# Decoder layer on one core: the seven products of a down part accumulate on copied-in sums and come in steps behind three tiles

## Chip, core and metric

The kernel runs on one core of a Trainium2 chip, as one program. The metric is the device time of one execution in microseconds (us). The core has a matrix engine (TensorE, PE in the profile, with its weight loads as PEld), a vector engine (VectorE, DVE), a scalar engine (ScalarE, ACT), GpSimd (POOL) and SyncE (SP). Each takes its instructions in the order in which they stand in its queue. In this kernel SP issues the plain transfers of the weights and POOL the others, among them transfers that add to what stands at their destination.

## The reference

One layer of a decoder: a SwiGLU block, a merge of attention and a linear recurrence, and a second SwiGLU block, each between two RMS norms. 512 tokens, model width 1024, 2816 hidden units in each SwiGLU block. The change touches the two SwiGLU blocks only:

```python
def swiglu(x, w_gate, w_up, w_down):
    return (jax.nn.silu(x @ w_gate) * (x @ w_up)) @ w_down

for l in range(DEPTH):
    f = swiglu(rms_norm(h, ffn1_norm_pre[l]), ffn1_w_gate[l], ffn1_w_up[l], ffn1_w_down[l])
    h = h + 0.5 * rms_norm(f, ffn1_norm_post[l])
    ...                      # attention, recurrence, merge
    f = swiglu(rms_norm(h, ffn2_norm_pre[l]), ffn2_w_gate[l], ffn2_w_up[l], ffn2_w_down[l])
    h = h + 0.5 * rms_norm(f, ffn2_norm_post[l])
```

## The kernel before

**Precision.** Every matrix product runs as three products of 32-bit operands that were split into a high and a low part (high times high, high times low, low times high). `split` (L277) makes the two parts of an operand: ACT copies the high part (L278), DVE subtracts it (L279). So each weight that the stream brings must pass ACT and DVE before PE can use it.

**Tiles and parts.** A SwiGLU block (`ffn`) has NF = 22 tiles f of 128 hidden units. The first ones (5 in the first block, 3 in the second) are plain products. From then on a tile is a `prod`: gate and up projection together, computed as a 2 by 2 block product with seven instead of eight block products (p1 to p7, `seven`, L592). One prod is 7 products of 12 matmuls of 256 columns (L603 to L605). Within it a partial sum b is copied to SBUF by ACT (`c`, L610) before the next product accumulates on it, and DVE forms the results g and u from PSUM and these copies (L615). The tiles fall into five parts (`FF_PARTS`): part 0 is tiles 0 to 3, parts 1, 2, 3 are four tiles each, part 4 is tiles 16 to 21.

**Down projection.** Part 0 and part 4 are projected down plainly. Parts 1 to 3 (`SEVEN`) use seven block products again: `down7` is called one tile late, behind tiles 8, 12 and 16. Its 14 groups (7 products, two token blocks each) of 6 matmuls of 512 columns (L783 to L785) go to PSUM. After each group ACT copies the partial sum to a tile `cs` (L789), and POOL issues one or two accumulating transfers (L791) that add it to the output sums `facc`: 16 for a part, 96 in the program. The seven operands on the weights' side are made by `d_forms` from two fetches of 1 MB, both ahead of tile 8 (12, 16); one sum is made by a further accumulating transfer (L743). Three of the seven are made in `rest`, in the middle of `down7`.

**What sets the order.** `ffn_order` writes the order of the events down; a scheduler then places the instructions on each engine, with priority for what is marked `high_priority`. The order of PE follows the events. The weights come as one stream in the order of `stream_plan`, at most 1 MB at a time, into two buffers `raw` (L222), issued by SP (L224). A fetch starts when the last instruction that reads the buffer's earlier content is done. The split weights stand in four tiles `w8` of [128, 2, 1024] and two `w4`. `w_forms` (L573) makes a prod's seven operands from 1 MB: four sums on DVE (L579, L580, L581, L584), three large splits and a small one; it takes three `w8`, so each waits until PE has used what stood there.

**PSUM.** Eight banks: five `acc`, three `aux`. A prod takes two `acc` and one `aux`.

**Other tiles named below.** The pool tag `wd` holds one tile: the split activations of tile 3 (`act3`) until part 0's down projection has run, and then the rows of gains for the norm behind the block, which POOL fetches (L409). The tag `tt` holds the unsplit forms of a down part's activations. `last_product` ends the block: part 4's down projection added to `facc`, and the norm. Its matmuls (L397 to L399) start behind tile 21; their weights go into spare tiles, `tx` among them.

## Time and profile before

| | |
|---|---|
| time, median of 3 runs | 1268.79 us (1265.55 to 1272.86) |
| the profiled execution's own time | 1275.29 us |
| its span, first to last instruction | 1273.5 us |
| busy: PE / DVE / ACT / POOL | 97% / 76% / 58% / 9% of the span |
| granted TensorE clock, mean | 0.987 |

The profile is one execution, 6.5 us above the median of the runs. Times within it count from the first instruction. A matmul's row shows more than the time from one start to the next, since matmuls overlap, so the pace of PE is read from starts. The first SwiGLU block's prods and down parts (tiles 5 to 21) stand at 82.65 to 328.87 us, the second's at 980.29 to 1226.30 us. In the view of waits, a line gives who waited for whom, the total, how often, and the longest. In the chain of waits each row is what the work that ended last was waiting for at that time.

### The profile page before, as it was taken

The numbers are of one execution on the slowest core, as the hardware profiler recorded it, in microseconds if no ns is written. First come the engines' busy times: TensorE is split into PE (matmuls) and PEld (weight loads), VectorE is DVE, ScalarE is ACT, GpSimd is POOL, SyncE is SP. The second block draws the span as 40 slices with busy tenths as digits, with TensorE's granted clock in tenths as the row PEclk, the third lists the DMA queues.
The fourth block names the chain that finished last, engine by engine and source line by source line (L and its number), as shares of the span: only waits on it lengthen the run. The fifth ranks groups of instructions, "written<-read, shape, count | busy, mean of one in ns | idle before, by whom it ended". The sixth has DMA issues, their size and how long they took to land.

```text
span 1273.5 us, 19380 instructions
## 1 busy us (share of the span) xinstructions
PE 1230.8 (97%) x7676; PEld 1114.4 (88%) x7676; DVE 971.4 (76%) x1521; ACT 735.1 (58%) x1214; POOL 113.4 (9%) x153
## 2 busy tenths in 40 slices
PE   9999999999999999999999999999999999989887
PEld 8889888989777899999988887888998989888886
DVE  7969697878577488888575888854885879787855
ACT  7546656565455455666543797634664575756442
POOL 0000314030002000000000000000100031313000
PEclk9999999999899999999999999999999999999889
DMA  6233859584535122222242222225533386858631
GB/s 237 100 105 111 198 150 209 140 199 134 196 116 158 66 108 80 96 77 98 98 167 99 94 74 97 102 97 182 161 122 115 103 204 153 202 140 187 157 133 66
DMA packets 42075, 169.72 MB, mean 133 GB/s; under 512 B 4608, under 2 KB 7808, under 8 KB 27904
## 3 DMA queue, kind: packets, MB, share of 16 engines
q1 hardware_dynamic: 20016, 122.86, 28.0%
q0 software_dynamic: 21968, 45.62, 16.5%
q8 instruction: 60, 0.98, 0.3%
q14 instruction: 31, 0.25, 0.1%
HBM read 129.67 MB, written 6.29 MB: 107 GB/s over the span
## 4 chain that ended last, share of the span: by engine, by line
PE 73%; DVE 12%; DMA 8%; ACT 5%; issue 2%; DVEq 0%; SPq 0%; ACTq 0%
PE acc L603 8%; PE acc L604 8%; PE acc L605 8%; DMA raw<-in_w 8%; PE acc L291 6%; PE acc L292 6%; PE acc L293 6%; DVE w L279 4%; PE acc L397 3%; PE acc L399 3%; PE acc L398 3%; PE acc L783 2%; PE acc L784 2%; PE acc L785 2%; PE aux L603 2%; PE aux L604 2%
## 5 line engine op out<-in xcount | busy, mean ns | idle before, releaser
L279 DVE TENSOR_TENSOR w<-raw,w 128x1024 fp32r<-128x1024 f32 (+1 forms) x279 | 304.0, 1094 | 105.5 <-ACT w L278 93.1
L278 ACT ACTIVATE w<-raw 128x1024 fp32r<-128x1024 f32 (+1 forms) x279 | 265.5, 954 | 155.4 <-PE acc L293 48.3
L603 PE MATMUL acc<-big,w 128*128 128x256 f32 x896 | 254.7, 284 | 0.6 <-ACT c L610 0.6
L604 PE MATMUL acc<-big,w 128*128 128x256 f32 x896 | 254.6, 284 | 0.0
L605 PE MATMUL acc<-big,w 128*128 128x256 f32 x896 | 254.1, 284 | 0.0
L603 PEld LDWEIGHTS acc<-big,w 128*128 128x128 f32 x896 | 172.1, 192 | 1.4 <-ACT c L610 0.9
L604 PEld LDWEIGHTS acc<-big,w 128*128 128x128 f32 x896 | 172.0, 192 | 0.4
L605 PEld LDWEIGHTS acc<-big,w 128*128 128x128 f32 x896 | 172.0, 192 | 0.0
L603 PE MATMUL acc<-tx,w 128*128 128x256 f32 x272 | 80.0, 294 | 24.1 <-ACT c L610 23.9
L791 POOL DMA_DIRECT2D facc<-cs x96 | 82.0, 872 | 152.7 <-ACT cs L789 75.8
L610 ACT ACTIVATE c<-acc 128x256 f32<-128x256 f32 x172 | 65.0, 378 | 49.8 <-PE acc L605 46.1
L603 PE MATMUL aux<-big,w 128*128 128x256 f32 x288 | 83.2, 289 | 0.0
L604 PE MATMUL aux<-big,w 128*128 128x256 f32 x288 | 83.1, 288 | 0.0
L605 PE MATMUL aux<-big,w 128*128 128x256 f32 x288 | 83.0, 288 | 0.0
L605 PE MATMUL acc<-tx,w 128*128 128x256 f32 x272 | 78.7, 289 | 0.0
L604 PE MATMUL acc<-tx,w 128*128 128x256 f32 x272 | 78.4, 288 | 0.0
L603 PEld LDWEIGHTS acc<-tx,w 128*128 128x128 f32 x272 | 53.5, 197 | 26.5 <-ACT c L610 26.5
L291 PE MATMUL acc<-big,w 128*128 128x512 f32 x192 | 74.7, 389 | 0.0
L292 PE MATMUL acc<-big,w 128*128 128x512 f32 x192 | 74.7, 389 | 0.0
L293 PE MATMUL acc<-big,w 128*128 128x512 f32 x192 | 74.7, 389 | 0.0
L579 DVE TENSOR_TENSOR s<-raw 128x512 f32<-128x512 f32 x52 | 35.9, 690 | 47.0 <-DMA raw<-in_w 46.9
L279 DVE TENSOR_TENSOR w<-s,w 128x1024 fp32r<-128x1024 f32 x52 | 63.5, 1221 | 2.8 <-ACT w L278 2.7
(352 smaller groups left out, 2982.7 us busy)
## 6 DMA issues: line engine op xcount, KB each, us to landing
raw<-in_w SPq DMA_DIRECT2D x110, 1024.0 KB, 4.8
facc<-cs POOLq DMA_DIRECT2D x96, 256.0 KB, 6.7
raw<-raw POOLq DMA_DIRECT2D x6, 512.0 KB, 4.4
big<-xf POOLq DMA_DIRECT2D x6, 512.0 KB, 4.5
gains<-in_rows POOLq DMA_DIRECT2D x5, 512.0 KB, 7.4
h<-in_x SPq DMA_DIRECT2D x8, 256.0 KB, 5.2
h<-in_xn POOLq DMA_DIRECT2D x4, 512.0 KB, 5.5
kept_m<-h POOLq DMA_DIRECT2D x4, 512.0 KB, 2.9
```

Of the source, the lines that this page charges most:

```text
L278: ACT.activation(dh, src, AF.Copy)
L279: DVE.tensor_sub(dl, src, dh.bitcast(F32))
L291: PE.matmul(ps, wh, xh, start=first, stop=False)
L292: PE.matmul(ps, wh, xl, start=False, stop=False)
L293: PE.matmul(ps, wl, xh, start=False, stop=last)
L397: PE.matmul(ps, x.hi[k][:, bl], wh, start=k == 0, stop=False)
L398: PE.matmul(ps, x.hi[k][:, bl], wl, start=False, stop=False)
L603: PE.matmul(ps, wh, xh, start=start and k == 0, stop=False, skip_group_check=True)
L604: PE.matmul(ps, wh, xl, start=False, stop=False, skip_group_check=True)
L605: PE.matmul(ps, wl, xh, start=False, stop=k == 3, skip_group_check=True)
L610: ACT.activation(c, ps, AF.Copy)
L791: nc.gpsimd.dma_start(fb(o + i, FHALVES[half]), c, accum_op=ALU.add)
```

## The change

Down7 is cut into three steps: products p1 and p7 behind the first tile of the next part, p4, p6 and p5 behind the second, p2 and p3 behind the third (`SEVEN_STEPS`). Each step fetches its own quarters of the weights (1 MB, 1 MB, 0.5 MB; the quarter u0 twice) and makes its operands on DVE (four additions a part instead of three and an accumulating transfer). The activations' forms are made together behind the part's fourth tile.

Nothing is accumulated by transfers any more. Each product has a sum in SBUF: p2, p3 and p4 have a quarter of `facc`, p1, p7, p6 and p5 have a place in a new tile `ea`. Ahead of a group ACT copies the sum into the PSUM bank (`seed`), the group's matmuls accumulate on it, and ACT copies it back. In part 1 the four products with a place in `ea` start from nothing. The first three seeds of a step are written ahead of the tile before it; each later one stands behind the copy back of the group that had the bank. Behind part 3, eight DVE additions of 128x1024 (`merge`) put the places in `ea` into `facc`: five behind its second step, three behind its third.

Down groups now use the three `aux` banks, part 0's too; a prod takes three `acc`. The fourth tile of part 0 moves to the tag `e`, and `wd` holds the steps' running sum `sum` of the weights, from part 1's first step to part 3's last. So the gains wait for that.

```diff
+SEVEN_STEPS = (("p1", "p7"), ("p4", "p6", "p5"), ("p2", "p3"))
+SEVEN_RAW = (("g0", "u0"), ("u1", "u0"), ("g1",))
...
 def ffn_order(n):
...
+    after = {FF_PARTS[a + 1][0] + i: (a, i) for a in SEVEN for i in range(len(SEVEN_STEPS))}
...
+        if f in after:
+            order.append(("prepd",) + after[f])
...
+        if f in after:
+            order.append(("seeds",) + after[f])
         order.append(("prod", f))
...
+        if f in after:
+            order.append(("down7",) + after[f])
...
-                for i in range(2):
-                    plan.append((("dg", n, ev[1], i), 2048))
+                for q in SEVEN_RAW[ev[2]]:
+                    plan.append((("dq", n, ev[1], q), 1024))
...
+            tt = x["tt"]
+            put(tt[:, i // 2 * 2:i // 2 * 2 + 2, i % 2, :], lambda ap: ap.rearrange("p (q t) -> p q t", q=2))
+            q = tt.rearrange("p q j t -> p q (j t)")
+
+            def pair(*ps):
+                v = f32r_big().rearrange("p (s c) t -> p s (c t)", s=2)
+                for k, p in enumerate(ps):
+                    x[p] = v[:, :, k * T:k * T + T]
+                return v
+
+            def form(v, src):
+                split(v[:, 0], v[:, 1], src)
+
+            if i == 1:
+                pair("p1", "p7")
+                form(x["p1"], q[:, 0])
+                DVE.tensor_sub(q[:, 0], q[:, 0], q[:, 1])
+            if i == 3:
+                with tc.high_priority(offset=AHEAD):
+                    DVE.tensor_sub(q[:, 1], q[:, 3], q[:, 1])
+                    form(x["p7"], q[:, 1])
+                    two = pair("p6", "p4")
+                    v = f32r_big().rearrange("p c t -> p (c t)")
+                    x["p5"] = v[:, 0:2 * T].rearrange("p (s t) -> p s t", s=2)
+                    form(x["p5"], q[:, 0])
+                    DVE.scalar_tensor_tensor(q[:, 0], q[:, 3], -1.0, q[:, 0], op0=ALU.mult, op1=ALU.subtract)
+                    DVE.scalar_tensor_tensor(q[:, 1], q[:, 0], -1.0, q[:, 2], op0=ALU.mult, op1=ALU.subtract)
+                    form(two, tt[:, 0:2].rearrange("p q j t -> p (q j t)"))
+                    form(pair("p2", "p3"), tt[:, 2:4].rearrange("p q j t -> p (q j t)"))
...
-                ps, y = acc_ps(), fb(b, FHALVES[half])
+                ps = aux_ps()
                 tokens(ps, ws, part(a), b)
-                if a == 0:
-                    ACT.activation(y, ps, AF.Copy)
-                else:
-                    DVE.tensor_add(y, ps, y)
+                ACT.activation(fb(b, FHALVES[half]), ps, AF.Copy)
 
         def prod(f, w):
             g, u = tmp("g"), tmp("u")
-            seven(t, w, aux_ps()[:, :HB], [g[:, h] for h in HALVES], [u[:, h] for h in HALVES])
+            seven(t, w, acc_ps()[:, :HB], [g[:, h] for h in HALVES], [u[:, h] for h in HALVES])
...
+        def d_forms(a, i):
+            x, w = sevens[a], {}
             def form(name, src):
                 w[name] = w8()
                 split(w[name][:, 0, :], w[name][:, 1, :], src)
             with tc.high_priority(offset=AHEAD):
+                raw = [raw_of(("dq", n, a, q)) for q in SEVEN_RAW[i]]
+                if i == 0:
+                    x["sum"] = apool.tile([P, 2, D], F32, name="sum", tag="wd", bufs=1)[:, 0, :]
+                sd = x["sum"]
+                if i == 0:
+                    g0, u0 = raw
+                    form("p1", g0)
+                    DVE.tensor_add(sd, g0, u0)
+                    form("p7", sd)
+                elif i == 1:
+                    u1, u0 = raw
                     form("p4", u1)
+                    DVE.tensor_add(sd, sd, u1)
+                    DVE.tensor_add(u0, u0, u1)
+                    form("p6", sd)
+                    form("p5", u0)
+                else:
+                    g1, = raw
+                    form("p2", g1)
+                    DVE.tensor_add(sd, sd, g1)
+                    form("p3", sd)
+            return w
...
+        outs = {"p2": (0, 0, 1.0), "p3": (2, 0, 1.0), "p4": (0, 1, -1.0)}
+        extra = ("p1", "p7", "p6", "p5")
+        seeded = {}
+        def quarter(o, half):
+            return facc.rearrange("p (b h) t -> p b h t", h=2)[:, o:o + 2, half, :]
+        def sum_at(p):
+            if p in outs:
+                o, half, sign = outs[p]
+                return quarter(o, half), sign
+            return acts["ea"][:, extra.index(p)], 1.0
+        def groups(i):
+            return [(p, k) for p in SEVEN_STEPS[i] for k in range(2)]
+        def seed(a, p, k):
+            if "ea" not in acts:
+                acts["ea"] = apool.tile([P, 4, 2, T], F32, name="ea", tag="e", bufs=1)
+            ps = seeded[p, k] = aux_ps()
+            if p in outs or a > SEVEN[0]:
+                src, sign = sum_at(p)
+                ACT.activation(ps, src[:, k], AF.Copy, scale=sign)
+        def down7(a, i, w):
+            x = sevens[a]
+            gs = groups(i)
+            for m, (p, k) in enumerate(gs):
+                ps = seeded.pop((p, k))
+                first = not (p in outs or a > SEVEN[0])
+                for j in range(2):
+                    xh, xl = (x[p][:, s_, j * HB + k * P:j * HB + k * P + P] for s_ in range(2))
+                    wh, wl = (w[p][:, s_, j * T:(j + 1) * T] for s_ in range(2))
+                    PE.matmul(ps, xh, wh, start=first and j == 0, stop=False, skip_group_check=True)
+                    PE.matmul(ps, xh, wl, start=False, stop=False, skip_group_check=True)
+                    PE.matmul(ps, xl, wh, start=False, stop=j == 1, skip_group_check=True)
+                dst, sign = sum_at(p)
+                with tc.high_priority(offset=EVAC):
+                    ACT.activation(dst[:, k], ps, AF.Copy, scale=sign)
+                    if m + 3 < len(gs):
+                        seed(a, *gs[m + 3])
+            if a == SEVEN[-1]:
+                merge(i)
+        def merge(i):
+            p1, p7, p6, p5 = (acts["ea"][:, k] for k in range(4))
+            if i == 1:
+                DVE.tensor_add(p6, p6, p1)
+                DVE.tensor_add(p7, p7, p6)
+                for p in (p7, p5):
+                    DVE.tensor_sub(quarter(2, 1), quarter(2, 1), p)
+                DVE.tensor_sub(quarter(0, 1), quarter(0, 1), p7)
+            if i == 2:
+                DVE.tensor_add(quarter(0, 0), quarter(0, 0), p1)
+                for p in (p6, p5):
+                    DVE.tensor_add(quarter(2, 0), quarter(2, 0), p)
...
+            elif ev[0] == "seeds":
+                for g in groups(ev[2])[:3]:
+                    seed(ev[1], *g)
...
             a = part_of(f)
             i = f - FF_PARTS[a][0]
-            if a:
-                if i % 2 == 0:
-                    acts[a, i // 2] = f32r_big()
-                at, i = acts[a, i // 2], i % 2
-            elif i == 3:
-                at, i = apool.tile([P, 4, T], F32R, name="act3", tag="wd", bufs=1), 0
...
```

The order on three engines. In these rows the number behind a tile's name is that of its buffer, and the line is that of the program the row is from: in the changed one L286 and L287 are the two halves of `split`, L587 to L592 the sums of `w_forms`, L618 and L623 the copies c and the sums g and u, L739 a tile's silu and L740 the product g times u behind it, L798 a seed, L814 a copy back, L824 to L832 the merges.

On DVE in the first block, before, around the first sum g of tile 20 (g_3127, from the bank acc_3131):

```order
L279 TENSOR_TENSOR w8_3114<-raw_3108,w8_3114 128x1024
L615 TENSOR_TENSOR g_3002<-aux_3004,c_3046 128x256
L584 TENSOR_TENSOR raw_3108<-s12_3110,raw_3108 128x512
L725 SCALAR_TENSOR_TENSOR u_3104<-g_3002,u_3003 128x512
L279 TENSOR_TENSOR w4_3117<-raw_3108,w4_3117 128x512
L615 TENSOR_TENSOR g_3127<-acc_3131,c_3144 128x256
```

And after, at the same sum (g_3115, from acc_3119):

```order
L287 TENSOR_TENSOR w8_3102<-raw_3096,w8_3102 128x1024
L830 TENSOR_TENSOR facc_79<-facc_79,ea_1134 128x2x512
L592 TENSOR_TENSOR raw_3096<-s12_3098,raw_3096 128x512
L287 TENSOR_TENSOR w8_3103<-s12_3098,w8_3103 128x1024
L832 TENSOR_TENSOR facc_79<-facc_79,ea_1134 128x2x512
L287 TENSOR_TENSOR w4_3105<-raw_3096,w4_3105 128x512
L287 TENSOR_TENSOR w8_3104<-raw_3096,w8_3104 128x1024
L832 TENSOR_TENSOR facc_79<-facc_79,ea_1134 128x2x512
L740 SCALAR_TENSOR_TENSOR u_3092<-g_2990,u_2991 128x512
L623 TENSOR_TENSOR g_3115<-acc_3119,c_3132 128x256
```

The sum g of tile 20 moved behind three merges and behind two more of tile 21's large splits. From the last split of tile 18's weights to this sum there stand 48 rows on DVE: 20 of 1024 columns a partition (8 of them merges), 19 of 512 and 9 of 256.

On ACT in the first block, before, from the last copy c of tile 21 (c_3306) on; g_3234 is tile 21's silu, tx_3473 a split of the last product's weights, xf_3231 the split of tile 21's activations:

```order
L610 ACTIVATE c_3306<-acc_3237 128x256
L278 ACTIVATE tx_3473<-raw_3468 128x1024
L724 ACTIVATE g_3234<-g_3234 128x512
L278 ACTIVATE act_3470<-raw_3468 128x1024
L278 ACTIVATE xf_3231<-u_3336 128x512
```

And after:

```order
L618 ACTIVATE c_3294<-acc_3225 128x256
L739 ACTIVATE g_3222<-g_3222 128x512
L286 ACTIVATE tx_3461<-raw_3456 128x1024
L286 ACTIVATE xf_3219<-u_3324 128x512
L286 ACTIVATE act_3458<-raw_3456 128x1024
```

The silu moved ahead of the split `tx` and the activations' split ahead of `act`; on DVE the product u behind the silu moved ahead of `tx` too. The second block ends in the same way.

On ACT in the first block, after, in the second step of part 2 (p4, p6, p5), from tile 13's silu on; sums are copied back and seeds copied in in turn with the forms of tile 14's weights:

```order
L739 ACTIVATE g_1970<-g_1970 128x512
L814 ACTIVATE facc_79<-aux_1964 128x512
L798 ACTIVATE aux_2084<-ea_1134 128x512
L814 ACTIVATE facc_79<-aux_1966 128x512
L286 ACTIVATE w8_1952<-s12_1947 128x1024
L798 ACTIVATE aux_2093<-ea_1134 128x512
L814 ACTIVATE ea_1134<-aux_1968 128x512
L286 ACTIVATE w4_1954<-raw_1945 128x512
L286 ACTIVATE w8_1953<-raw_1945 128x1024
L798 ACTIVATE aux_2102<-ea_1134 128x512
```

Before, ACT copied sums to `cs` between such forms and had no seeds. In the second step of parts 2 and 3 the last group, on the bank of the last seed above, stands on PE behind the first 5 matmuls of the next tile. On POOL the 48 transfers `facc<-cs` and 3 `raw<-raw` of each block are gone, and the gains are the only transfers there between a block's first tiles and its end.

More of the change, by code (lines that the diff above doesn't have):

```diff
@@ L646, in act_at @@
             i = f - FF_PARTS[a][0]
[L647 to L653 removed]
+            if a == 0:
                 if i == 0:
@@ L656, in act_at @@
                 at = acts[0]
+            else:
+                if i == 0:
+                    acts[a] = apool.tile([P, 4, T], F32R, name="act4", tag="tt", bufs=1)
+                elif i % 2 == 0:
+                    acts[a] = f32r_big()
+                at, i = acts[a], i % 2
             acts["at", f] = at[:, 2 * i, :], at[:, 2 * i + 1, :]
@@ L670, in into @@
                 u = tmp("u")
-                put(u)
+                put(u, lambda ap: ap)
                 split(*act_at(f), u)
@@ L694, in into @@
-            DVE.scalar_tensor_tensor(tt[:, 2, :], tt[:, 1, :], -1.0, u[:, :HB], op0=ALU.mult, op1=ALU.subtract)
-            x["t", j] = f32r_big().rearrange("p s t -> p (s t)").rearrange("p (s k t) -> p s k t", s=2, k=4)
-            split(x["t", j][:, 0], x["t", j][:, 1], tt)
+                sevens[a] = {"tt": apool.tile([P, 4, 2, HB], F32, name="tt", tag="tt", bufs=1)}
+            x = sevens[a]
+            tt = x["tt"]
+            put(tt[:, i // 2 * 2:i // 2 * 2 + 2, i % 2, :], lambda ap: ap.rearrange("p (q t) -> p q t", q=2))
@@ L708, in std_out @@
             DVE.tensor_mul(u, psu, r)
-            into(f, lambda dst: DVE.tensor_mul(dst, u, g))
+            into(f, lambda dst, v: DVE.tensor_mul(dst, v(u), v(g)))
         def down(a, half):
@@ L819, in ffn @@
             elif ev[0] == "down7":
-                down7(ev[1], *forms.pop("d"))
+                down7(*ev[1:], forms.pop("d"))
             else:
```

108 lines of the change are left out of this document (16 added, 92 removed).

## The prediction, made before the changed kernel ran

> **What bounds the kernel now.** I read the page first, then the stretch of each SwiGLU block from tile 5 to tile 21, then PE's waits in it, then the chain of waits behind one of them.
>
> ```profile
> PE 1230.8 (97%) x7676; PEld 1114.4 (88%) x7676; DVE 971.4 (76%) x1521; ACT 735.1 (58%) x1214; POOL 113.4 (9%) x153
> raw<-in_w SPq DMA_DIRECT2D x110, 1024.0 KB, 4.8
> facc<-cs POOLq DMA_DIRECT2D x96, 256.0 KB, 6.7
> ```
>
> PE is the bound. What is to be won is the time in which it waits. A weight fetch of 1 MB lands 4.8 us behind its issue (median).
>
> ```profile
> 82.65:328.87 246.22, 233.12 (x1681) 221.99 (x1680) 203.20 (x288) 150.67 (x238) 46.97 (x57) 0.99 0.66 170
> 980.29:1226.30 246.01, 234.51 (x1681) 223.03 (x1680) 202.58 (x287) 150.47 (x238) 46.28 (x56) 0.98 0.66 168
> 299.61 0.42 DVE L615 TENSOR_TENSOR g<-aux,c 128x256 f32<-128x256 f32 x1
> 309.69 0.41 DVE L615 TENSOR_TENSOR g<-aux,c 128x256 f32<-128x256 f32 x1
> 124.69 0.40 PE L783 MATMUL acc<-w,xf 128*128 128x512 f32 x1
> 143.76 0.28 PE L603 MATMUL acc<-big,w 128*128 128x256 f32 x1
> ```
>
> The first two rows are the stretches of tiles 5 to 21 in the two blocks: length, then busy time of PE, PEld, DVE, ACT, POOL. The next two are the last sums of two undisturbed tiles: a tile is 309.69 - 299.61 = 10.08 us of PE, so a product (a seventh) is 1.44. The last two are the first matmul of a down7 and the first behind it: 19.07 us for 14 groups, 1.36 a group. Seventeen tiles and three down7 make 17 x 10.08 + 3 x 19.07 = 228.6 us. The stretches take 246.2 and 246.0: **17.6 and 17.4 us are lost** in them.
>
> ```profile
> PE acc L603 <- ACT c L610: 13.0, 5, 3.3
> PE acc L603 <- ACT c L610: 11.4, 6, 3.7
> 226.00:229.40 3.40, 3.40 (x18) 3.40 (x17) 2.89 (x6) 1.85 (x4) 0.00 (x0) 0.50 1.02 292
> 229.40:232.80 3.40, 3.40 (x31) 3.40 (x30) 3.00 (x4) 1.72 (x3) 0.00 (x0) 1.00 0.30 54
> ```
>
> PE's waits in the two stretches are 13.0 us in 5 and 11.4 us in 6, nearly all on the copy c. Behind a wait of over 3 us the granted clock is 0.50 for a while: 18 matmuls instead of 31 in 3.40 us, which is 13 x 0.12 = 1.5 us more.
>
> ```profile
> 212.08 7.27 DMA raw<-in_w
> 219.38 0.70 DVE s L579
> ...
> 224.34 0.34 DVE g L615
> 224.71 0.63 ACT g L724
> 225.34 0.28 ACT c L610
> 212.56 0.85 POOL L791 DMA_DIRECT2D facc<-cs  x1 [0.37 <-issue]
> 213.83 0.85 POOL L791 DMA_DIRECT2D facc<-cs  x1 [0.42 <-DMA facc<-cs]
> ```
>
> The first five rows are the chain behind part 2's down7; they end a wait. The weights of tile 15 land after 7.27 us instead of 4.8. DVE has their sums in its queue ahead of tile 13's last sums, so those come late; ACT has tile 13's silu ahead of tile 14's copy c; PE waits for c. The fetch is late twice over: it starts late, since down7 held both buffers, and it shares the transfer engines with `facc<-cs`, which POOL issues at 212.56 and 213.83 (the last two rows).
>
> **What the change does, term by term.** The 96 accumulating transfers and their six sisters go, and with them the bursts: fetches should land in about 4.8 us. A part's 2 MB of down weights come in three fetches over three tiles, so no tile's fetch waits behind `rest`. I went through ACT, DVE and the buffers for parts 1 to 3 with the durations of this trace, and found each tile's weights split 2 us or more ahead of their first matmul. The waits behind down7 go with what follows them.
>
> ```profile
> 83.14 1.20 POOL L409 DMA_DIRECT2D gains<-in_rows  x2 [82.70 <-PE acc L399]
> 83.89 7.05 DMA raw<-in_w
> 96.92 0.28 ACT c L610
> ```
>
> The first wait of each stretch stands ahead of down7 (its c at 96.92) and comes from another neighbour: the gains are fetched at 83.14, and the weight fetch at 83.89 takes 7.05 us. Now the gains wait for the tag `wd`, until part 3's last step, so this one goes too. All of 17.6 and 17.4 goes, then; what comes in its place:
>
> (1) **Merges on DVE.** Eight additions a block.
>
> ```profile
> L754 DVE TENSOR_TENSOR raw<-sd,raw x6: 1221/1222/1222, 126.5 to 1150.6; 128x1024 f32<-128x1024 f32 x6
> 285.76 1.22 DVE L279 TENSOR_TENSOR w<-raw,w 128x1024 fp32r<-128x1024 f32 x1
> 286.89 0.42 DVE L615 TENSOR_TENSOR u<-acc,c 128x256 f32<-128x256 f32 x1
> 287.23 1.22 DVE L279 TENSOR_TENSOR w<-raw,w 128x1024 fp32r<-128x1024 f32 x1
> 295.23 0.69 DVE L580 TENSOR_TENSOR s<-s,raw 128x512 f32<-128x512 f32 x1
> 295.84 0.69 DVE L581 TENSOR_TENSOR raw<-raw 128x512 f32<-128x512 f32 x1
> ```
>
> An addition of 128x1024 in SBUF (L754) lasts as long as a large split, and from start to start a large split takes 286.89 - 285.76 = 1.13 us, a row of 512 0.61 and one of 256 0.34. From the last split of tile 18 to the first sum g of tile 20, the 48 rows on DVE take 20 x 1.13 + 19 x 0.61 + 9 x 0.34 = 37.2 us. They begin when the second group of p6 is done and ACT has made the high part (1.05, and 0.5 for what stands ahead of it). From that group on, PE has 2 groups, tile 18, 4 groups, tile 19 and five products of tile 20: 2.7 + 10.1 + 5.4 + 10.1 + 7.2 = 35.5 us, less 1.5 that DVE starts later, 34.0. The product p4 of tile 20 overwrites the bank that this sum g reads. So PE waits about **3.2 us** there; queued behind p4 is the rest of the tile. Without the merges (8 x 1.13 = 9.0) there would be 5.8 us to spare. Bounds: 0 if DVE falls back less, some 6 if its splits wait for ACT. I add 1.5 for the clock, as behind the wait that ended behind 225.34: 4.7 a block.
>
> The Trainium skill ("TensorE: Matmul & The Clock Gate", section on what is actually happening) says that the clock halves after at least one idle window of about 3.4 us and that the windows run freely. The trace agrees for the wait that ended behind 225.34. By that rule a wait of 3.2 us would mostly keep the clock, and the sum would be 1.5 us a block lower.
>
> (2) **Seeds and copies back on ACT.** No row shows ACT writing PSUM. The nearest is the copy the other way:
>
> ```profile
> L789 ACT ACTIVATE cs<-acc x60: 577/597/601, 126.3 to 1165.4; 128x512 f32<-128x512 f32 x60
> ```
>
> I take 0.6 us; bounds 0.3 (the copy c of half the width) and 1.05 (a split of twice the width). 34 seeds a block add 20 us to 151 of ACT in some 230, which fits. 11 of them stand within a step, each behind a copy back, while PE has two more groups (2.7 us) ahead: 0.6 + 0.6 fits, with a form of 1.05 between them too. Only the last seed of the second step stands behind two forms; there PE has 5 matmuls of the next tile put ahead (0.6 us). I count 0.3 for each of two places: 0.6 a block, bounds 0 and 4.
>
> (3) DVE's extra addition a part (1.2 us) and the refetched quarter (0.5 MB a part) lie beside PE: DVE has 203 of 246 us busy and gets 3.6 + 9.0 more, in some 236. What that cover costs when it fails is term 1. I count 1.5 a block for small waits of the kind that the stretch shows already (17.6 - 13.0 - two times 1.5 leaves 1.6).
>
> So 4.7 + 0.6 + 1.5 = 6.8 a block in place of 17.6 and 17.4: **-10.8 and -10.6**.
>
> (4) **The end of each block.**
>
> ```profile
> 324.49 7.84 DMA raw<-in_w
> 332.35 1.07 ACT tx L278
> 334.58 0.69 DVE u L725
> 335.30 0.64 ACT xf L278
> 335.99 0.79 PE acc L397
> PE acc L397 <- ACT xf L278: 6.3, 2, 3.2
> 335.99:342.00 6.01, 6.01 (x14) 4.75 (x15) 3.54 (x5) 1.62 (x3) 0.00 (x0) 0.50 0.48 174
> ```
>
> ACT waits until 332.35 for a fetch, and tile 21's silu stands behind that split; so its product u comes at 334.58, its split at 335.30, and PE has waited 3.2 us (6.3 in the two blocks) and then has half its clock for 6 us: 14 matmuls where 0.227 a matmul would give 26, some 2.8 us. Now silu and u stand ahead of `tx`. If the fetch lands as before, xf's high part begins at 333.3 and is there at 333.9 instead of 335.9, and its low part, behind `tx` on DVE, at about 335.3: two short waits, 2.1 us in all, and the clock stays. That is 3.2 + 2.8 - 2.1 = **-3.9** a block, bounds -1.1 (the clock falls all the same) and -6.
>
> Sum: 10.8 + 10.6 + 7.8 = 29.2. The profiled execution, 1275.3 us, would come to 1246; from the median of 1268.8, 6.5 lower, **1240 us**.
>
> **Rivals.**
>
> *The merges cost nothing.* DVE was idle 43 us in each stretch, so it may be less far behind than I add up: 2 x 4.7 less, 1230. Against it: the idle time lies in waits that now go.
>
> *Half of it comes back.* Seeds, copies c and forms in one queue cost more than 0.6: at 0.7 us for each of the 22 seeds within a step, 15 us, 1255.
>
> *The change doesn't do what it says.* PE's waits would come from two buffers for a stream, not from the bursts. If fetches still took 7.3 us, a tile's sums would come 2.5 later, and with a margin of about 1 each of the 18 steps would wait 1.5: 27 us, 1267, no change. Against it: the fetches of 7.05 and 7.27 us shown above stand beside the gains and `facc<-cs`, and the median is 4.8.
>
> *Slower.* Place: the seed within a step. ACT stands in order, and a seed behind a form waits as long as the form does. In this trace ACT waits like that:
>
> ```profile
> 161.49 0.63 ACT L724 ACTIVATE g<-g 128x512 f32<-128x512 f32 x1 [4.18 <-DVE g L615]
> 171.88 0.64 ACT L724 ACTIVATE g<-g 128x512 f32<-128x512 f32 x1 [2.27 <-DVE g L615]
> ```
>
> If each of 22 seeds came 2.3 us late, 50 us, it would be 1290. It decides from 29 / 22 = 1.3 us a seed, one group's length. For it: 34 seeds a block that PE never waited for before. Against: the forms between them wait for PE's own groups, which are done.
>
> **How the numbers follow.** Forecast 1240 (from 1233 to 1249): 0.48. Merges free, 1230: 0.14. Half comes back, 1255: 0.18. No change, 1267: 0.12. Slower, 1290: 0.08. The range leaves out the last two: 1228 (merges free, clock kept) to 1262. About 0.5%, 6.3 us, is what a measurement of this kernel can tell from no change: faster 0.80, same 0.12, slower 0.08.
>
> **What would show it.** The list of waits: no wait of tiles 9, 10, 14 and 17 on c behind down7; fetches at 4.8 us; a wait of about 3 us of PE at tile 20 on DVE's sum g. If PE waits for ACT within the steps at L809, the seeds are mis-sized; if it waits for c again, the landing was not the cause. At a block's end PE's wait should fall from 3.2 to about 2, with the clock at 1.

## The result, and the profile after

| | before | after |
|---|---|---|
| median of 4 runs each (before: one more than at the prediction) | 1269.55 us (1265.55 to 1272.86) | 1234.06 us (1233.44 to 1234.56) |
| ratio after / before | | 0.9722, 95% interval 0.9692 to 0.9751 |
| the profiled execution's own time | 1275.29 us | 1234.56 us |
| its span | 1273.5 us | 1232.8 us |
| granted TensorE clock, mean | 0.987 | 0.999 |

The change takes 35.5 us off the median and 40.7 us off the profiled execution. The profiled execution of before lies 5.7 us above its median and that of after 0.5 us above its own, which is the difference between the two.

The page after: busy time of each engine, the row of POOL's queue (packets, MB, share of 16 engines' span) and the row of the weight fetches (count, KB each, median us from issue to landing).

```profile
PE 1217.3 (99%) x7676; PEld 1103.6 (90%) x7676; DVE 987.9 (80%) x1513; ACT 767.3 (62%) x1276; POOL 26.1 (2%) x51
q0 software_dynamic: 7280, 17.30, 4.1%
raw<-in_w SPq DMA_DIRECT2D x110, 1024.0 KB, 4.8
```

ACT does 32 us more and DVE 16 us more than before, and both lie beside PE, which is now busy 99% of the span. The median over all 110 fetches is 4.8 us, as it was: it hides what changed. The same median for the fetches issued from 82 to 330 us alone, before:

```profile
DMA to landing us min/median/max: 4.7/6.8/8.9
```

and after:

```profile
DMA to landing us min/median/max: 3.4/4.8/7.4
```

In the first block's stretch the median was 2 us above that of the whole program (in the second block's it was 6.0, 1.2 above), and now it is 4.8 in both. (The 3.4 is a fetch of half the size.)

The two stretches of tiles 5 to 21 after, by the view of windows (length, then PE, PEld, DVE, ACT, POOL busy, granted clock, DMA share, GB/s):

```profile
83.39:312.51 229.12, 229.12 (x1682) 218.75 (x1680) 212.13 (x286) 167.55 (x270) 3.29 (x6) 1.00 0.37 130
960.19:1189.31 229.12, 229.12 (x1682) 218.76 (x1681) 211.73 (x286) 167.55 (x270) 2.66 (x5) 1.00 0.35 128
```

246.2 and 246.0 us have become 229.1 twice, 0.5 us over the 228.6 that PE's own pace gives. PE is busy all of the time and the clock stands at 1.00. What follows tile 21 up to the mixer, and in the second block up to the end of the program, is 3.6 and 3.7 us shorter. What PE still waits for in the SwiGLU blocks stands in the view of waits (total, times, longest):

```profile
PE acc L405 <- ACT xf L286: 3.1, 2, 1.7
PE acc L407 <- DVE xf L287: 0.8, 2, 0.4
```

All of it is at the two block ends. No line is left of the 24.5 us that PE waited for the copy c, and there is none for a sum of DVE, which the prediction had put at tile 20.

### The profile page after: what moved, and what is told of

Its sections match the earlier page's. It is cut to its first block, busy times and chain, and to the rows that moved or that the text cites. A ratio compares the mean times of both kernels' runs of the same rounds, so it can differ in the third digit from the quotient of the medians.

```text
span 1232.8 us, 19128 instructions
## 1 busy us (share of the span) xinstructions
PE 1217.3 (99%) x7676; PEld 1103.6 (90%) x7676; DVE 987.9 (80%) x1513; ACT 767.3 (62%) x1276; POOL 26.1 (2%) x51
## 3 DMA queue, kind: packets, MB, share of 16 engines
q0 software_dynamic: 7280, 17.30, 4.1%
## 4 chain that ended last, share of the span: by engine, by line
PE 87%; DVE 6%; ACT 4%; DMA 1%; issue 1%; DVEq 0%; ACTq 0%
PE acc L611 14%; PE acc L612 14%; PE acc L613 14%; PE acc L299 6%; PE acc L300 6%; PE acc L301 6%; PE aux L809 3%; PE aux L810 3%; PE aux L811 3%; PE acc L407 2%; PE acc L406 2%; PE acc L405 2%; PE aux L406 1%; PE aux L405 1%; PE aux L407 1%; DMA raw<-in_w 1%
## 5 line engine op out<-in xcount | busy, mean ns | idle before, releaser
L287 DVE TENSOR_TENSOR w<-raw,w 128x1024 fp32r<-128x1024 f32 (+1 forms) x273 | 295.8, 1089 | 98.3 <-ACT w L286 88.0
L286 ACT ACTIVATE w<-raw 128x1024 fp32r<-128x1024 f32 (+1 forms) x273 | 257.9, 950 | 138.5 <-PE acc L301 48.3
L612 PE MATMUL acc<-big,w 128*128 128x256 f32 x1184 | 335.9, 284 | 0.0
L613 PE MATMUL acc<-big,w 128*128 128x256 f32 x1184 | 335.6, 284 | 0.0
L611 PE MATMUL acc<-big,w 128*128 128x256 f32 x1184 | 335.4, 284 | 0.0
L611 PEld LDWEIGHTS acc<-big,w 128*128 128x128 f32 x1184 | 226.7, 192 | 1.0
L612 PEld LDWEIGHTS acc<-big,w 128*128 128x128 f32 x1184 | 226.8, 192 | 0.8
L613 PEld LDWEIGHTS acc<-big,w 128*128 128x128 f32 x1184 | 226.8, 192 | 0.2
L618 ACT ACTIVATE c<-acc 128x256 f32<-128x256 f32 x208 | 79.0, 380 | 74.7 <-PE acc L613 68.8
L611 PE MATMUL acc<-tx,w 128*128 128x256 f32 x272 | 77.2, 284 | 0.0
L612 PE MATMUL acc<-tx,w 128*128 128x256 f32 x272 | 77.0, 283 | 0.0
L613 PE MATMUL acc<-tx,w 128*128 128x256 f32 x272 | 76.9, 283 | 0.0
L286 ACT ACTIVATE w<-s 128x1024 fp32r<-128x1024 f32 x52 | 55.1, 1060 | 27.3 <-PE acc L613 21.6
L809 PE MATMUL aux<-w,xf 128*128 128x512 f32 x168 | 66.1, 393 | 0.0
L287 DVE TENSOR_TENSOR w<-s,w 128x1024 fp32r<-128x1024 f32 x52 | 63.5, 1220 | 2.9 <-ACT w L286 2.7
L810 PE MATMUL aux<-w,xf 128*128 128x512 f32 x168 | 65.6, 390 | 0.0
L811 PE MATMUL aux<-w,xf 128*128 128x512 f32 x168 | 65.4, 389 | 0.0
L299 PE MATMUL acc<-xf,w 128*128 128x512 f32 (+1 forms) x152 | 52.9, 354 | 0.0
L301 PE MATMUL acc<-xf,w 128*128 128x512 f32 (+1 forms) x152 | 52.3, 345 | 0.0
```

The source lines that it names most:

```text
L286: ACT.activation(dh, src, AF.Copy)
L287: DVE.tensor_sub(dl, src, dh.bitcast(F32))
L299: PE.matmul(ps, wh, xh, start=first, stop=False)
L301: PE.matmul(ps, wl, xh, start=False, stop=last)
L611: PE.matmul(ps, wh, xh, start=start and k == 0, stop=False, skip_group_check=True)
L612: PE.matmul(ps, wh, xl, start=False, stop=False, skip_group_check=True)
```

## Experiments

Each ratio is to the kernel before, timed beside the experiment on the same chip. The changed kernel itself was not timed again beside them. Its 1234.06 us belongs to the comparison above, where before took 1269.55 us against 1270.58 to 1272.18 here, so a difference of one or two microseconds from it can't be told. The length of a wait of PE is that of its row or of the view of waits.

### What did the gain come from: the transfers, the steps, or the seeds?

**The kernel before without its 96 transfers** (the sums of down7 never reach the output).

```diff
-                    for o, half in outs:
-                        nc.gpsimd.dma_start(fb(o + i, FHALVES[half]), c, accum_op=ALU.add)
```

> The kernel before without the 96 transfers facc<-cs, which leaves the sums of parts 1 to 3 out of the output. Theory: both halves count, transfers beside the fetches and the order that holds both buffers: fetches land in 4.8 us again, the waits behind down7 shrink by about 2.5 each and lose the clock's share, but some stay: 1245 to 1255. Rival A (transfers alone): all waits behind down7 go, some 30 us: 1238 to 1243. Rival B (buffers and order alone): 1266 to 1270.

Measured: 1241.56 us (1239.69 to 1243.46) against 1272.18, ratio 0.9764 (0.9742 to 0.9786), 30.6 us less. PE's waits in the first stretch:

```profile
PE acc L603 <- ACT c L610: 1.6, 1, 1.6
```

Before, there were five of these, 13.0 us. The one that is left is the first, beside the fetch of the gains. Down7 still stands in one piece behind one tile, still holds both `raw` buffers and still has `rest` in its middle, and no tile behind it waits. So the removed transfers alone give most of the gain, 30.6 of 35.5 us, and that a tile's fetch starts late behind down7 costs nothing by itself. The theory, that both halves count, gave 1245 to 1255 and fell; rival A holds. What is left to the change stands in the two first waits (1.6 and 0.8 us) and at the block ends, where PE still waits 3.4 and 2.6 us, with a granted clock of 0.50 and 0.75 over the 6 us behind.

**The steps with the transfers.** The changed kernel with its three steps, its fetches and its DVE sums, but each group goes out by the 96 transfers again, from eight places in `ea`, instead of by seeds and merges (some sums are left out).

```diff
-                ACT.activation(ps, src[:, k], AF.Copy, scale=sign)
...
-                    ACT.activation(dst[:, k], ps, AF.Copy, scale=sign)
+                    ACT.activation(c, ps, AF.Copy, scale=sign)
...
+                for o, half in tos:
+                    nc.gpsimd.dma_start(fb(o + k, FHALVES[half]), c, accum_op=ALU.add)
```

> The changed kernel's steps behind three tiles, but each group's sum is copied to a tile and added to facc by 16 accumulating transfers a part, as before; no seeds, no merges; the shared sums are left out of the output. Theory: fetches land in 6 to 7 us and the margin of 1 to 2 us covers most of it; some waits come back: 1238 to 1250. Rival A (transfers were all): 1258 and more. Rival B (only the burst in order counted): 1234 within 2.

Measured: 1265.86 us (1262.48 to 1269.44) against 1270.58, ratio 0.9960 (0.9941 to 0.9980). The fetches from 82 to 330 us in this kernel:

```profile
DMA to landing us min/median/max: 3.5/6.4/9.3
```

and PE's waits on c in the whole program:

```profile
PE acc L611 <- ACT c L618: 13.6, 9, 2.7
```

Spread over three tiles, the transfers slow the fetches about as much as they did in one burst (a median of 6.4 us instead of 6.8 here, 6.5 instead of 6.0 in the second block's stretch), and PE waits for c at nine places, and at three more for a copy to `ea` (2.0 us). The chain behind one of these waits has the same head as before:

```profile
165.19 7.84 DMA raw<-in_w
```

The steps without the removal are worth 4.7 us, 0.4%, and a part of this can be the gains, which come late in this kernel too. PE waits less for c than before (13.6 us instead of 24.5), so it isn't ruled out that a late start makes a slow fetch dearer.

**The removal without the spreading.** The changed kernel with seeds, copies back and merges, but all three steps of a part back to back behind its first tile.

```diff
-    after = {FF_PARTS[a + 1][0] + i: (a, i) for a in SEVEN for i in range(len(SEVEN_STEPS))}
+    after = {FF_PARTS[a + 1][0]: (a, 0) for a in SEVEN}
...
+            for i in range(1, len(SEVEN_STEPS)):
+                order += [("prepd", after[f][0], i), ("seeds", after[f][0], i), ("down7", after[f][0], i)]
```

> The changed kernel with a part's three steps back to back behind the first tile; sums still copied in by ACT, no accumulating transfers. Theory: spreading the steps is needed, since a step's weights must be fetched (4.8 us) and split (4 and more) while PE has 5.4 to 8.2 us of the step before: waits of 3 to 6 us at most steps, 18 steps: 1260 to 1300. Rival (the transfers were all): 1234 to 1240.

Measured: 1236.82 us (1234.97 to 1237.95) against 1270.58, ratio 0.9728 (0.9712 to 0.9745). That can't be told from the change itself (0.9722, 0.9692 to 0.9751). The stretches, 83.00 to 313.00 and 960.00 to 1189.30:

```profile
83.00:313.00 230.00, 230.00 (x1681) 218.96 (x1680) 211.50 (x287) 166.26 (x270) 3.28 (x6) 1.00 0.36 129
960.00:1189.30 229.30, 229.30 (x1676) 218.31 (x1675) 210.79 (x284) 166.49 (x270) 2.66 (x5) 1.00 0.35 125
```

The theory's waits, 3 to 6 us at most steps, did not come: PE never waits in these stretches either, though 2.5 MB are fetched and made into forms for one step of 14 groups. The spreading over three tiles, which the change's name speaks of, is not what makes it fast.

**No seeds.** The changed kernel without the 68 copies into PSUM; every group starts from nothing, so sums of earlier parts are lost.

```diff
-                ACT.activation(ps, src[:, k], AF.Copy, scale=sign)
...
-                first = not (p in outs or a > SEVEN[0])
+                first = True
```

> The changed kernel without the seeds: every group starts from nothing, so that only part 3's sums reach the output. Theory: the seeds stand beside PE's work and cost nothing: 1234 within 1.5. Rival: ACT holds PE up by them, 1 to 2 us a block: 1230 to 1232.

Measured: 1234.75 us (1232.94 to 1235.13) against 1270.58, ratio 0.9709 (0.9691 to 0.9727), the time of the change. ACT's busy time falls from 767 to 734 us and nothing follows from it: the seeds cost nothing that can be told here.

### Is it the adding, or any transfer?

By the pages, POOL's queue took 16.5% of the engines' time for 45.62 MB before and takes 4.1% for 17.30 MB after. So the accumulating transfers took 12.4% for 28.3 MB, against 28.0% for the 122.86 MB of the weights' queue, and a byte that is added looks about twice as dear. The kernel before with the 96 transfers as plain writes (the output sums of parts 1 to 3 are not formed):

```diff
-                        nc.gpsimd.dma_start(fb(o + i, FHALVES[half]), c, accum_op=ALU.add)
+                        nc.gpsimd.dma_start(fb(o + i, FHALVES[half]), c)
```

> The kernel before, in which the 96 transfers of down7 stay, at the same size and in the same places, but write instead of adding (so the output sums of parts 1 to 3 are not formed). Left out altogether they bring 30.6 us (1241.56 against 1272.18). Theory: what slows the weight fetches is the adding: by the page's queue rows the 102 accumulating transfers move 28.3 MB in 12.4% of 16 engines' span, half as many bytes per engine time as the weights' queue (122.86 MB in 28.0%). Then plain writes take half the engine time and most of the loss goes: 1245 to 1256, and the fetches of the stretches land in a median of 5 to 5.7 us instead of 6.1 to 6.8. Rival: any 256 KB transfer at that moment does it, whatever its kind: 1262 to 1275, fetches at 6 us or more. If the waits of PE come from the order of the program and not from the transfers: also 1262 to 1275, but with fetches below 5.5.

Measured: 1271.2 us (1267.63 to 1279.46) against 1271.65, ratio 0.9999 (0.9971 to 1.0026). My theory fell. The plain writes are cheaper for the transfer engines, as their rows on this kernel's page show:

```profile
q0 software_dynamic: 15824, 45.62, 10.4%
...
facc<-cs POOLq DMA_DIRECT2D x96, 256.0 KB, 4.2
```

16.5% have become 10.4%, and they land in 4.2 us instead of 6.7. The fetches' median in the stretches falls too, to 5.9 and 5.0. PE's time doesn't follow, since the fetches that count are the slow ones right beside down7. The chain behind the wait that ended at 225.4 us:

```profile
199.82 9.15 DMA raw<-in_w
...
212.66 6.44 DMA raw<-in_w
...
224.45 0.63 ACT g L724
225.08 0.28 ACT c L610
...
225.40 0.58 PE acc L603
```

9.15 and 6.44 us beside writes that add nothing. In the second stretch, where the median is 5.0, two of the chains still start with fetches of 8.29 and 5.73 and of 9.56 and 5.97 us. So the median of 5.0 does not speak for the third reading, in which the order of the program makes PE wait; and with the transfers out, that order made PE wait no more.

One more rival is settled by this run. Before, ACT had to wait for a transfer now and then until a tile `cs` was free again; in the first stretch:

```profile
ACT cs L789 <- DMA facc<-cs: 3.0, 4, 1.0
```

In the second stretch it was 4.3 us. With the plain writes no such wait is left in either stretch, and the time is the same. So it is the traffic of these transfers beside the fetches, whether they add or write. The Trainium skill ("DMA: Bandwidth & Descriptors", section on queues, rings and completion order) says that each transfer engine takes turns between the queues that have work, a packet at a time. That fits a 1 MB fetch slowing from 4.8 to between 6 and 9 us beside 256 KB transfers of either kind; these runs show the slowing, not the turns.

### The wait at tile 20 that did not come

**The changed kernel without its merges** (four of the seven products are left out of the output).

```diff
-            if a == SEVEN[-1]:
-                merge(i)
```

> The changed kernel without the eight merges a block; the sums in ea are left out of the output. Theory: DVE falls 3.5 us behind at tile 20 as forecast, but PE has tile 20's p3 and 19 matmuls of tile 21 in its queue ahead of p4 and never waits, so the merges cost nothing: 1234 within 1.5. Rival (term 1 of the prediction): the merges cost 3 to 5 a block: 1225 to 1228.

Measured: 1237.87 us (1236.87 to 1239.55) against 1271.90, ratio 0.9739 (0.9704 to 0.9774). No gain over the change: the first block's tiles 5 to 21 take 229.2 us (82.58 to 311.78), where the change takes 229.1, so at tile 20 there was nothing to win. If anything it is slower, at the block's end, where its chain runs:

```profile
307.40 8.01 DMA raw<-in_w
...
315.42 1.07 ACT tx L286
...
316.51 1.23 DVE tx L287
317.74 0.61 DVE u L740
...
318.38 0.64 ACT xf L286
```

With DVE less loaded the scheduler puts tile 21's product u behind the split of `tx` again, as in the kernel before, and PE waits 3.2 us, with a granted clock of 0.75 over the 6 us behind it.

**Twice the merges** (eight more additions of the same size a block, on places that are read no more).

```diff
+                for _ in range(5):
+                    DVE.tensor_add(p7, p7, p6)
...
+                for _ in range(3):
+                    DVE.tensor_add(p7, p7, p6)
```

> The changed kernel with eight more additions of 128x1024 a block, behind the merges (9.0 us of DVE; their results are not used). Theory: DVE is some 12 us behind at tile 20; matmuls of the next tile cover a part, the rest shows as waits in tiles 19 to 21 or at the block's end, 3 to 8 a block: 1240 to 1250. Rival: DVE has room: 1234 within 1.5.

Measured: 1239.54 us (1239.46 to 1239.86) against 1271.90, ratio 0.9751 (0.9710 to 0.9792). PE's waits on DVE's sum g:

```profile
PE acc L611 <- DVE g L623: 4.7, 2, 2.4
```

9.0 us more of DVE a block cost about 2.7 in all. The wait is there now, 2.4 us a block with a clock of 0.69 over the 5.5 us behind the first, but the order of PE has moved p4 of tile 20 still further back, behind five products of tile 21. Against it, the waits at the two block ends are gone from this kernel's list.

**The order of PE, pinned.** So I read PE's order in the changed kernel at this place, which I had not done for the prediction (number of matmuls, product):

| kernel before, and the code | the changed kernel |
|---|---|
| 12 of p4, tile 20 | 12 of p3, tile 20 |
| 12 of p3, tile 20 | 12 of p1, tile 21 |
| 12 of p1, tile 21 | 7 of p2, tile 21 |
| 12 of p2, tile 21 | 12 of p4, tile 20 |

The scheduler has put 31 matmuls, 31 x 0.12 = 3.7 us, ahead of p4. DVE's lag is nearly as predicted: its rows in the changed kernel around the sum g of tile 20 are

```profile
299.82 1.22 DVE L287 TENSOR_TENSOR w<-raw,w 128x1024 fp32r<-128x1024 f32 x1
300.96 1.22 DVE L832 TENSOR_TENSOR facc<-facc,ea 128x1024 f32<-128x1024 f32 x1
302.10 0.69 DVE L740 SCALAR_TENSOR_TENSOR u<-g,u 128x512 f32<-128x512 f32 x1
302.70 0.42 DVE L623 TENSOR_TENSOR g<-acc,c 128x256 f32<-128x256 f32 x1
```

Tile 20 begins at 292.33, so after five products p4 would have been due at 292.33 + 7.2 = 299.53, and the sum is done at 302.70 + 0.42 = 303.12: 3.6 us late, where I had predicted 3.2. The 3.7 us of other matmuls cover it, with 0.1 us to spare. To show that, this kernel holds p3 of tile 20 behind its p4, and tile 21 behind that:

```diff
-        product("p4", y, True)
+        end = product("p4", y, True)
...
-        product("p3", z, False)
+        with tc.issue_after(end.ins) if pinned else ExitStack():
+            end = product("p3", z, False)
...
+            with tc.issue_after(acts["end"].ins) if f == NF - 1 else ExitStack():
+                acts["end"] = seven(t, w, acc_ps()[:, :HB], [g[:, h] for h in HALVES], [u[:, h] for h in HALVES],
+                                    pinned=f == NF - 2)
```

> The changed kernel with PE's order pinned in tiles 20 and 21: p3 of tile 20 behind its p4, tile 21 behind p3. Theory: DVE's sum g of tile 20 stays 3.2 to 3.5 us behind p4, now with nothing ahead of p4; PE waits that long in each block, and 1.5 more where the clock falls: 1240.5 to 1244. Rival: DVE isn't behind and the order on PE is of no account: 1234 within 1.5, no wait at tile 20.

Measured: 1248.3 us (1247.17 to 1249.6) against 1271.90, ratio 0.9820 (0.9784 to 0.9856); by its ratio some 12 us above the change, more than expected. PE's rows at p4 of tile 20 (in brackets the idle time ahead and what ended it):

```profile
298.65 0.28 PE L613 MATMUL acc<-big,w 128*128 128x256 f32 x1
302.40 0.58 PE L611 MATMUL acc<-big,w 128*128 128x256 f32 x1 [3.47 <-DVE g L624]
```

and the window behind that wait in the same kernel:

```profile
302.40:308.00 5.60, 5.59 (x34) 5.60 (x35) 2.88 (x5) 1.34 (x2) 0.00 (x0) 0.70 0.36 152
```

The wait of term 1 is there, 3.5 us, and behind it a clock of 0.70 for 5.6 us, 1.7 us of loss: 5.2 a block, where term 1 had 4.7. The rest of the 12 us is the block's end, where PE waits 3.4 and 2.4 us instead of 2.1 and 1.8, the second time with the clock down (0.72 over the 6 us behind it). The forecast of 1240.5 to 1244 had left that out.

### The first wait and the block's end

**Gains late, in the kernel before.** `sd` of part 3 takes the tag `wd`, so POOL's fetch of the gains waits as it does in the change.

```diff
+                if a == SEVEN[-1]:
+                    sd = apool.tile([P, 2, D], F32, name="late", tag="wd", bufs=1)[:, 0, :]
```

> The kernel before with a sum of part 3's weights under the tag wd, so that the gains wait for it. Theory: the fetch at 83.9 lands in 4.8 instead of 7.05 us, and the first wait of each block (1.6 and 1.1) is gone from the trace; the others stay. Rival: that wait comes from something else and stays.

Measured in a single run: 1268.15 us, 4.0 below the median of before (1272.18) and 0.9 below the fastest of its nine runs, so the time says little; the trace says more. The weight fetch beside the old place of the gains lands in 5.1 us instead of 7.05, and of PE's waits only those behind down7 are left in the stretches; the first wait of each (1.5 and 0.9 us) is gone:

```profile
PE acc L603 <- ACT c L610: 21.3, 10, 3.0
```

**Tail order, in the kernel before and in the changed one.** The splits of the last product's spare weights are held behind tile 21's split `xf`, on ACT and on DVE. The same edit in both:

```diff
+                with ExitStack() as late:
+                    if behind and half and kk:
+                        for ins in behind:
+                            late.enter_context(tc.issue_after(ins.ins))
+                    ws.append(fetch(key(half, kk), slots.pop(0) if half else None))
...
-                split(*act_at(f), u)
+                acts["last"] = split(*act_at(f), u)
```

> The kernel before with tile 21's silu and the split of its activations put ahead of the splits tx and act. Theory: the order there is the cause of the 3.2 us of waiting and the 2.8 of half clock: both go in both blocks, some 12 us: 1256 to 1260. Rival: PE waits for the fetch itself; no change: 1266 to 1271.

Measured in the kernel before: 1262.92 us (1260.19 to 1264.43) against 1272.18, ratio 0.9929 (0.9909 to 0.9949), 9.3 us less, where some 12 had been expected; the waits for xf have left the list, and those on c are as before (24.5 us in 12).

> The changed kernel with the split of tile 21's activations put ahead of the splits tx and act of the last product's weights on ACT and DVE. Theory: the 2.4 us that PE still waits at each block's end come from these splits standing ahead while their fetch lands; they go: 1229 to 1230. Rival: PE waits for something else there (the silu's own chain): 1234.

Measured in the changed kernel: 1229.19 us (1228.86 to 1229.62) against 1271.90, ratio 0.9670 (0.9636 to 0.9704). This is the fastest of all kernels here, about 4.9 us below the change. The waits of PE at the two block ends, 2.1 and 1.8 us (2.4 and 2.1 from start to start of the matmuls), are gone. ACT at the end of the first block now:

```profile
312.73 0.63 ACT L745 ACTIVATE g<-g 128x512 f32<-128x512 f32 x1 [2.95 <-DVE g L629]
314.12 0.63 ACT L286 ACTIVATE xf<-u 128x512 fp32r<-128x512 f32 x1 [0.76 <-DVE u L746]
314.66 1.04 ACT L286 ACTIVATE tx<-raw 128x1024 fp32r<-128x1024 f32 x1
```

In the change `tx` stood between silu and xf, and waited 2.31 us for its fetch.

**The rows of h later, in the kernel before.** POOL's four fetches of 512 KB for the norm start behind the first half of the last product and not ahead of it.

```diff
-    for b in range(4):
-        nc.gpsimd.dma_start(hb(b), xN[b])
...
+                if after is not None and not half and b == 0:
+                    held(after)
```

> The kernel before with the block's four loads of h held back until the first sum of the last product is made (by a copy of one column each on DVE). Theory: the fetch at 324.5 lands in 7.84 us because these loads run beside it; alone it lands in 4.8, ahead of tile 21's silu, and PE waits no more than 0.5 at a block's end: 1256 to 1260. Rival: the fetch is slow for another reason; 7 to 8 us and no change.

Measured: 1262.54 us (1257.45 to 1266.65) against 1272.18, ratio 0.9930 (0.9906 to 0.9954), 9.6 us less, but not by the way that was forecast. In the first block the order is as before, and the last fetch lands in 6.66 us instead of 7.84, not in 4.8. PE's wait falls from 3.1 to 1.9 us, and the clock still falls behind it, to 0.72 over 6 us (19 matmuls, against 14 before and 26 at the full clock):

```profile
327.48 6.66 DMA raw<-in_w
337.80:343.80 6.00, 6.00 (x19) 4.79 (x20) 3.79 (x9) 1.62 (x3) 0.77 (x2) 0.72 0.52 175
```

So the loads of h explain 1.2 of the 3.0 us by which that fetch was late. POOL moves nothing beside the 6.66; what overlaps it is another weight fetch of the same queue, issued 2.9 us later, which lands in 6.4 us.

In the second block PE's wait is gone, but there ACT's order has changed:

```profile
1224.72 0.63 ACT L726 ACTIVATE g<-g 128x512 f32<-128x512 f32 x1 [2.82 <-DVE g L617]
1226.11 0.63 ACT L278 ACTIVATE xf<-u 128x512 fp32r<-128x512 f32 x1 [0.76 <-DVE u L727]
1229.79 2.94 ACT L278 ACTIVATE big<-raw 128x1024 fp32r<-128x1024 f32 x3
```

Tile 21's silu and the split of its activations now stand ahead of the splits `big`, as the experiment on the tail order had put them. So this run doesn't show what the loads of h cost in the second block.

## Why the prediction was right, and where not

The forecast was 1240 us; the median is 1234.06, inside the range. By its own steps, against the profiled execution:

- **All of 17.6 and 17.4 goes: right, and for the reason given**, but the reason had two halves and only one is needed. "It shares the transfer engines" is shown as far as this: with the transfers out the time falls by 30.6 us, and with plain writes in their place nothing is gained. "It starts late, since down7 held both buffers", and with it "three fetches over three tiles, so no tile's fetch waits behind `rest`", is refuted as a cause of its own: with the transfers out, neither the old down7 in one piece nor the three steps in one piece make PE wait behind down7. Whether a late start makes a slow fetch dearer is not separated (24.5 us of waits on c before, 13.6 with the steps and the transfers). The rival "two buffers, not bursts" falls with it.
- **Term 1, the merges on DVE, 4.7 a block: this is the step that failed.** "PE waits about 3.2 us there; queued behind p4 is the rest of the tile" took PE's order at tile 20 from the code. DVE's part of the sum was right to 0.4 us. But PE's order there has 3.7 us of other matmuls ahead of p4, so PE waits 0. I had read DVE's order for this term and not PE's. Pinned to the code's order, the wait comes: 3.5 us and 1.7 us of clock. The rival "merges cost nothing" was right about the size, for a reason that it did not name.
- **The rule on the clock beside term 1.** By the rule of the Trainium skill ("TensorE: Matmul & The Clock Gate", section on what is actually happening) that the prediction quotes, a wait of 3.2 us would mostly keep the clock. The runs don't bear that out: pinned, the wait of 3.5 us did not keep it (0.70 over 5.6 us), while one of 3.4 us at the same kernel's first block end did; and waits of 2.4 us (that kernel's second block end) and 1.9 us (rows of h later, first block end) lost it too, both to 0.72 over 6 us. The 1.5 us that the sum took for the clock, 1.7 in the pinned kernel, was right.
- **Seeds, 0.6 a block: too much.** Their duration was right, 0.600 us against 0.6 taken; nothing waits for them, and without them the time is the same. The rivals "half comes back" and "slower" fall with that.
- **Small waits, 1.5 a block: too much.** Terms 1 and 2 and the small waits together were 6.8 a block, and 0.5 was measured. No wait of that kind is left in the stretches of the change, nor behind down7 in the kernel before without its transfers.
- **The block's end, -3.9: right**, -3.6 and -3.7, with two short waits in each, 2.1 and 1.8 us in all where 2.1 was forecast, and the clock at 1.
- **The gains**: right; the first wait of each stretch goes when they are late, and only then.

Stretches and block ends were to give 29.2; they gave 17.1 + 16.9 + 3.6 + 3.7 = 41.3, and the start of the program lost 0.7. The median moved 5.2 us less than the profiled execution, since that one was slow before. So the error of 11.5 in the sum showed as only 6 in the forecast, which is luck.

Open: why DVE's load makes the scheduler choose these orders was not tried, only what they do. And what the transfer engines do with two transfers at a time, of two queues or of one, is seen here only in landing times.

## What to carry over

Where PE waits for a stream of weights, look at the landing times of the fetches inside the stretch where it waits, not at the median of the page, and then at what else moves data at that time, on another queue or on the same one: taking those transfers away was worth most of this change, and spreading the steps out was worth next to nothing. When a wait is forecast from one engine's lag, read the order of the engine that is to wait as well: what stands ahead of the waiting instruction may cover the lag. And hold what ends a stage ahead of what only prepares the next one in the same queue; here that was worth 5 to 9 us by itself.

## What the runs showed of the hardware that was not expected

- Beside plain transfers of 256 KB the slowest 1 MB fetches are as slow as beside accumulating ones (up to 9.1 and 9.6 us in the two stretches, against 8.9 and 8.6, and a median of 4.8 in the whole program), although the plain ones hold the engines for much less time (10.4% instead of 16.5% with all of POOL's others) and land in 4.2 us instead of 6.7. The median fetch in the stretches does gain, from 6.8 and 6.0 to 5.9 and 5.0.
- Two overlapping 1 MB fetches of one queue, with no other queue's transfers beside them, landed in 6.7 and 6.4 us (rows of h later, first block end).
- The clock behind a wait went both ways. In the pinned kernel a wait of 3.5 us was followed by a granted clock of 0.70 and one of 3.4 us, at its first block end, by 1.00; in the kernel before, one of 3.0 us (ended at 289.8) was followed by 0.66 over 3.4 us and one of 3.1 us (at 162.5) by 1.00. Waits of 2.4 and 1.9 us at a block's end were followed by 0.72 over 6 us, and the change's of 1.7 us by 1.00. So a forecast of a wait of 2 to 3.5 us should carry the clock's loss as a chance, not as a yes or no.
- A copy of 128x512 by ACT takes the same time into PSUM (0.600 us) as out of it (0.597 us).
